# Turning the state-space values without TensorE, a third of the weight remainders on GpSimd, and a later row product in a two-layer hybrid decoder trunk

## The chip, the cores and the metric

The kernel runs on one core of a Trainium2 chip. The metric is the device time of one execution in microseconds (us), the median of several runs. Five engines work side by side, each with a queue of its own that it runs in order: TensorE (PE; its weight loads are listed as PEld), VectorE (DVE), ScalarE (ACT), GpSimd (POOL) and SyncE (SP), which here only issues DMAs. They wait for one another through semaphores. A name with a q behind it (SPq, ACTq) is the sequencer of that engine, which issues a DMA or waits.

## What is computed

Two layers run on a sequence of 512 rows of width 1024, in float32. Each layer norms its input, multiplies it by one large matrix, feeds four groups of heads, gates and joins them, multiplies by an output matrix, norms and adds.

```python
hn = rmsnorm(x, pre_g)
proj = hn @ w_in                                  # 1024 -> 6664
y_ret = retention(...) * silu(ret_g)
y_ssd = ssd_mixer(xbc, z, dt_raw, ...)            # state-space heads
y_sb  = stick_breaking(...) * silu(sb_g)
y_mem = memory_read(...) * silu(mem_g)
y = concatenate([y_ret, y_ssd, y_sb, y_mem]) @ w_out
return x + rmsnorm(y, post_g)

# in ssd_mixer, after the convolution and silu:
xs, bm, cm = split(xbc)
xdt = x_heads * delta                              # the values, by position
y_diag = einsum('bclsgj,bcsgjp->bclgjp', cb * decay_in, xdt)
states = einsum('bclgn,bclgjp->bcgjpn', bc, xdt * decay_states)
y = (y_diag + y_off) + x_heads * d_skip
y = rmsnorm((y * silu(z)) per group of 256, norm_g)
```

## The kernel before

Every float32 product of the large matrices is made of three matmuls. A tensor is held as a high part, rounded to the form that TensorE reads in one pass (fp32r), and a low part, the remainder (`x - high`); the product is high·high + high·low + low·high (`mm3`). ScalarE makes the high part by a copy (line 293), VectorE the low part by a subtraction (line 294), both in `split`.

**Weights.** They come from DRAM in 39 blocks a layer, each of two halves of 128 x 1024 (a few of 128 x 528); `w_load` loads a block of two into one of two `raw` buffers, `w_prefetch` splits a half into `wh` and `wl`. Halves are numbered k = 0 to 155 over both layers, 78 a layer. There are five buffers of `wh` and of `wl`, so half k can be split when half k-5 has been used, and in `proj_b` one half feeds 24 matmuls of 128 x 512. After an odd half has been split, its `raw` buffer is loaded anew from ScalarE's queue (line 353).

**Units.** `tick` counts one unit for each projection; `defer(n, f)` puts a step off until n units later. `ssd_group` (line 958) runs twice in each layer: two projections with a convolution make the values `X["x"]` (features by positions), further ones make B, C and the gates z. `ssd_values` (line 994) turns the values to positions by features: for each of two halves, four transposes of 128 x 128 on TensorE into a PSUM bank (line 1003), then VectorE multiplies by the step sizes into `xdt` (line 1007) and by the decay into `xds` (line 1009). `ssd_states` uses `xds` on TensorE one unit after the group's last projection, `ssd_out` uses `xdt` three units after it. `ssd_var` sums the squares over rows by a matmul and turns the row into reciprocal roots in `row_rstd` (ScalarE copy, DMA to 32 partitions, GpSimd add and power, DMA to DRAM, DMA back to all partitions); `ssd_norm` (line 1072) multiplies by them.

`columns_turned` (line 652) is the other way to turn a tile, used for B and for retention's keys: VectorE transposes blocks of 32 x 32 into a buffer (line 660), four DMAs put the 32-row strips into DRAM so that the blocks stand where they belong (line 663), and one DMA for each output reads it back (line 668), all on SP's queue.

`out_proj` multiplies the joined 16 tiles of 128 rows by the output matrix, column half by column half. In its first half tile kc is used by 12 matmuls; tiles 12 to 15 are the state-space outputs. At the end of layer 0 each quarter of the rows is normed (GpSimd adds and takes the power, lines 444, 449, 450), scaled (VectorE, line 470) and turned on TensorE (line 479) for the next layer.

Outside `start`, the order in each engine's queue is laid when the program is built, by a planner that takes whatever its own clock holds ready, in the order in which the steps are written (`schedule_with_timeline_sim=True`). Buffers come in tags with a fixed number of slots: "s" 33, "y" 16, "r" 9.

Of the kernel before, what the change touches and what calls it, by code (L numbers as in the profile page):

```python
# [8 lines left out]
F32 = mybir.dt.float32  # L9
# [7 lines left out]
P = 128  # L17
# [52 lines left out]
NBLK = len(BLOCKS)  # L70
# [4 lines left out]
def block_width(b):  # L75
    return 2 * (SUBD if BLOCKS[b % NBLK][0] == "d" else SUBW)
# [77 lines left out]

BLK = 32
TT = "y"
ST, SL, SB1, SB2 = "s", "y", 2, 4
ROW = 128  # L160

# [9 lines left out]
def v3(ap, a):  # L171
    return ap.rearrange("p (a b) -> p a b", a=a)


class Builder:
# [136 lines left out]
    def w_prefetch(self, upto=None, between=()):  # L312
        if self.starting and upto is None:
            return
        while self.w_split < (upto or min(self.nsubs, self.w_cur + self.NSUB)):
            k = self.w_split
            self.w_load(k // 2)
            n = block_width(k // 2) // 2
            h, l = (self.wp.tile([P, SUBW], F32R, tag=t, name=self.name(t), bufs=self.NSUB)[:, :n] for t in ("wh", "wl"))
            r = self.raw[k // 2]  # L320
            if isinstance(r, list):
                pieces = [(r[2 * (k % 2) + i][:], slice(512 * i, 512 * i + 512)) for i in range(2)]
            else:
                cs = [slice(0, n)] if k > 1 else [slice(0, n // 2), slice(n // 2, n)]
                pieces = [(r[:, (k % 2) * n + c.start:(k % 2) * n + c.stop], c) for c in cs]
            for i, (x, c) in enumerate(pieces):
                self.split(x, h[:, c], l[:, c], h[:, c].bitcast(F32))
                if i < len(between):
                    between[i]()
            self.sub[k] = (h, l)  # L330
            self.w_split += 1
            if k % 2:
                del self.raw[k // 2]
                if not self.starting:
                    self.w_load(k // 2 + self.NRAW)

    def w_load(self, b):
        while self.w_dma <= min(b, DEPTH * NBLK - 1):
            n = block_width(self.w_dma)
            src = self.a["wts"][self.w_off:self.w_off + P * n].rearrange("(p n) -> p n", p=P)  # L340
            if self.starting and self.w_dma == 2:
                r = [self.new(512, F32, "y") for _ in range(4)]
                for i in range(4):
                    self.nc.sync.dma_start(r[i][:], src[:, 512 * i:512 * i + 512])
            else:
                r = self.wp.tile([P, 2 * SUBW], F32, tag="raw", name=self.name("raw"), bufs=self.NRAW)
                if self.starting:
                    for c in ((slice(0, n),) if self.w_dma > 1 else (slice(0, n // 2), slice(n // 2, n))):
                        self.nc.sync.dma_start(r[:, c], src[:, c])  # L349
                        if not self.w_dma and not c.start:  # L350
                            self.mem_start()
                else:
                    self.nc.scalar.dma_start(r[:, :n], src)
            self.raw[self.w_dma] = r
            self.w_dma += 1
            self.w_off += P * n
# [273 lines left out]
    def mem_turn(self, h, w, y):  # L630
        nc = self.nc
        pT = []
        for m in range(2):
            T = self.buf(tag="y")
            for i in range(2):
                x = w[i].rearrange("p (t m j b) -> p m t j b", t=2, m=2, b=BLK)[:, m]
                nc.vector.transpose(T.rearrange("p (j t b) -> p t j b", t=NT, b=BLK)[:, 2 * i:2 * i + 2], x)
            d = self.turned_rows(P, SEQ)
            dd = d.rearrange("(j m) (a t) -> a m j t", m=BLK, a=P // BLK)
            pT.append(self.through_dram(T, dd, d, self.buf(tag="y")))  # L640
# [5 lines left out]
    def through_dram(self, T, dst, src, out):  # L646

        n = dst.shape[2]
        for a in range(P // BLK):
            self.nc.sync.dma_start(dst[a], v3(T[BLK * a:BLK * a + BLK], n))  # L650
        self.nc.sync.dma_start(out, src)
        return out

    def columns_turned(self, tiles, out):
# [3 lines left out]
        for k, x in enumerate(tiles):  # L658
            T = self.buf(n, TT)
            self.nc.vector.transpose(T, x)  # L660
            dd = d[:, P * k:P * k + P].rearrange("(b t) (a f) -> a t b f", t=BLK, a=P // BLK)
            for a in range(P // BLK):
# [296 lines left out]
    def ssd_group(self, l, g, ysb):  # L959

        X = {"l": l, "g": g}
        self.ssd_decay(X)
        X["x"] = [self.conv(self.proj_b(), 2 * g + i) for i in range(2)]
        self.defer(2, self.ssd_values, X)
        self.gated(("sb", 2 * g), ysb[2 * g])
        X["b"] = self.conv(self.proj_b(), 4 + g)
        X["bt"] = self.buf()[:, :3 * P]
        self.columns_turned([X["b"][:, :3 * P]], [X["bt"]])
        X["c"] = self.conv(self.proj_b(), 6 + g)
        self.defer(3, self.ssd_mix, X)  # L970
        self.gated(("sb", 2 * g + 1), ysb[2 * g + 1])
        X["y"] = [self.buf(tag="y"), self.buf(tag="y")]
        X["z"] = [self.gate(self.proj_b()) for _ in range(2)]
        self.defer(1, self.ssd_states, X)
        self.defer(3, self.ssd_out, X, 0)
        self.defer(3, self.ssd_out, X, 1)
        self.defer(5, self.ssd_var, X)
        self.defer(9, self.ssd_norm, X)

    def ssd_decay(self, X):  # L980
        nc, S = self.nc, self.ssd
# [12 lines left out]
    def ssd_values(self, X):  # L994

        nc, g = self.nc, X["g"]
        X["xdt"], X["xds"] = [], []
        for i in range(2):
            b = self.mx()
            for c in (2 * i, 2 * i + 1):  # L1000
                for j in range(2):
                    o = 256 * (c % 2) + P * j
                    nc.tensor.transpose(b[:, o:o + P], X["x"][j][:, P * c:P * c + P], self.con("ident", P))  # L1003
            xdt, xds = self.buf(), self.buf()
            for c in (2 * i, 2 * i + 1):
                s = slice(256 * (c % 2), 256 * (c % 2) + 256)
                nc.vector.tensor_tensor(out=v3(xdt[:, s], 4), in0=v3(b[:, s], 4), in1=self.per_head("delta", g, c), op=ALU.mult)
                if c < NT - 1:
                    nc.vector.tensor_tensor(out=v3(xds[:, s], 4), in0=v3(xdt[:, s], 4), in1=self.per_head("dst", g, c), op=ALU.mult)
            X["xdt"].append(xdt)  # L1010
            X["xds"].append(xds)
# [323 lines left out]
```

## Time and profile before

| | before |
|---|---|
| median of 3 runs | 924.06 us (923.71 to 925.14) |
| the profiled execution | 923.25 us |
| its span | 921.5 us |
| TensorE busy | 913.2 us, 99% |
| VectorE busy | 673.3 us, 73% |
| ScalarE busy | 443.5 us, 48% |
| GpSimd busy | 146.3 us, 16% |
| TensorE's granted clock | 0.998 of full speed |

The profile is of one execution. Its span is the time from the first instruction to the last; the execution's own time is 1.75 us longer. An engine is busy while it has an instruction in hand; matmuls overlap, each listed 0.39 us long for 512 columns but started 0.227 us apart, so what one costs is read from the start of the next.

### The profile page before, as it was taken

To read this page: it belongs to the slowest core of one execution; us is meant where nothing else is said; L and a number is where in the kernel's file an instruction comes from. 1 tells how busy PE (TensorE), PEld (TensorE's weight loads), DVE (VectorE), ACT (ScalarE), POOL (GpSimd) and SP (SyncE) were. 2 spreads that over 40 slices of the span, in tenths; PEclk is the share of its full clock that TensorE was granted. 3 is DMA by queue.
4 is the path that set the end of the run, shared out by engine and by line. 5 is a ranking of instruction groups with operands and counts; after the bars stand their busy time and mean duration, and the time that the engine had idled before them with its cause. 6 is when DMAs were issued, how large, how long until landed. Compare 5 with 4: busy or idle time off the path is not lost.

```text
span 921.5 us, 12952 instructions
## 1 busy us (share of the span) xinstructions
PE 913.2 (99%) x4667; PEld 773.6 (84%) x4667; DVE 673.3 (73%) x1081; ACT 443.5 (48%) x841; POOL 146.3 (16%) x208
## 2 busy tenths in 40 slices
PE   9999999999999999999999999999999999999997
PEld 7998888888888888888899888888888888888885
DVE  6855689888787887844587476898778869687343
ACT  6643485744453342733465336675445434335341
POOL 1200152320131110100040002423112120102001
PEclk9999999999999999999999999999999999999999
DMA  8544664642444333444345256556333362422502
GB/s 316 213 141 144 169 167 104 199 146 61 120 134 148 116 109 126 137 149 158 116 173 196 93 172 183 124 122 183 103 109 116 110 194 92 139 95 88 210 12 91
DMA packets 105408, 128.53 MB, mean 139 GB/s; under 512 B 64640, under 2 KB 79744, under 8 KB 96256
## 3 DMA queue, kind: packets, MB, share of 16 engines
q10 hardware_dynamic: 10224, 73.44, 23.4%
q1 hardware_dynamic: 95120, 54.28, 20.7%
q8 instruction: 36, 0.59, 0.3%
q14 instruction: 28, 0.23, 0.1%
HBM read 112.10 MB, written 15.56 MB: 139 GB/s over the span
## 4 chain that ended last, share of the span: by engine, by line
PE 98%; DMA 1%; ACT 0%; DVEq 0%; SPq 0%; POOLq 0%; issue 0%; POOL 0%; ACTq 0%; DVE 0%
PE pj L285 74%; PE mx L285 23%; PE mx L479 1%; DMA mem<-memT 1%; PE mx L1003 0%; ACT s L523 0%; DVEq L1331 0%; ACT s L1168 0%; POOLq L1331 0%; ACT wh L293 0%; SPq L506 0%; SPq L349 0%; SPq L1206 0%; POOL t L449 0%; ACTq L1331 0%
## 5 line engine op out<-in xcount | busy, mean ns | idle before, releaser
L285 PE MATMUL pj<-hTh,wh 128*128 128x512 f32 x704 | 276.4, 393 | 0.0
L285 PE MATMUL pj<-hTh,wl 128*128 128x512 f32 x704 | 275.8, 392 | 0.0
L285 PE MATMUL pj<-hTl,wh 128*128 128x512 f32 x704 | 274.6, 390 | 0.0
L294 DVE TENSOR_TENSOR wl<-raw,wh 128x1024 fp32r<-128x1024 f32 (+2 forms) x156 | 188.6, 1214 | 116.9 <-ACT wh L293 115.7
L293 ACT CAST wh<-raw 128x1024 fp32r<-128x1024 f32 (+2 forms) x156 | 158.7, 1020 | 205.0 <-PE pj L285 177.5
L285 PEld LDWEIGHTS pj<-hTh,wl 128*128 128x128 f32 x704 | 132.2, 188 | 27.3
L285 PEld LDWEIGHTS pj<-hTh,wh 128*128 128x128 f32 x704 | 132.3, 188 | 27.1 <-DVE s L593 0.8
L285 PEld LDWEIGHTS pj<-hTl,wh 128*128 128x128 f32 x704 | 132.3, 188 | 26.6
L285 PE MATMUL pj<-wh,s 128*128 128x512 f32 x320 | 97.6, 391 | 0.0
L285 PE MATMUL mx<-s,s 128*128 128x256 f32 (+4 forms) x528 | 79.7, 307 | 0.0
L285 PE MATMUL mx<-wh,s 128*128 128x512 f32 x256 | 79.2, 389 | 0.0
L285 PEld LDWEIGHTS mx<-s,s 128*128 128x128 f32 (+1 forms) x528 | 65.8, 177 | 8.2 <-PE pj L285 1.4
L285 PEld LDWEIGHTS pj<-wh,s 128*128 128x128 f32 x320 | 59.7, 188 | 12.4
L285 PE MATMUL pj<-wl,s 128*128 128x512 f32 x160 | 60.2, 389 | 0.0
L285 PEld LDWEIGHTS mx<-wh,s 128*128 128x128 f32 x256 | 48.1, 188 | 10.0
L294 DVE TENSOR_TENSOR s<-y,s 128x512 fp32r<-128x512 f32 x64 | 41.2, 687 | 19.7 <-ACT s L293 14.0
L262 ACT ACTIVATE s<-s 128x128 f32<-128x128 f32 (+3 forms) x96 | 41.8, 478 | 22.3 <-DVE s L733 20.6
L675 POOL TENSOR_TENSOR s<-y,s 128x512 fp32r<-128x512 f32 x16 | 23.7, 1494 | 179.9 <-ACT s L674 179.4
L293 ACT CAST s<-y 128x512 fp32r<-128x512 f32 x64 | 36.6, 617 | 30.8 <-PE mx L285 22.0
L285 PE MATMUL mx<-wl,s 128*128 128x512 f32 x128 | 49.6, 389 | 0.0
L285 PE MATMUL pj<-wl,hTh 128*128 128x256 f32 (+2 forms) x144 | 47.6, 331 | 0.0
L285 PE MATMUL pj<-wh,hTl 128*128 128x256 f32 (+2 forms) x144 | 47.5, 330 | 0.0
(185 smaller groups left out, 1298.5 us busy)
## 6 DMA issues: line engine op xcount, KB each, us to landing
raw<-wts ACTq DMA_DIRECT2D x69, 1024.0 KB, 4.8
s<-x SPq DMA_DIRECT2D x24, 256.0 KB, 4.1
y<-turned SPq DMA_DIRECT2D x24, 256.0 KB, 2.8
turned<-y SPq DMA_DIRECT2D x64, 64.0 KB, 2.2
s<-acs SPq DMA_DIRECT2D x16, 256.0 KB, 6.3
r<-row SPq DMA_DIRECT2D x12, 256.0 KB, 5.0
raw<-wts SPq DMA_DIRECT2D x4, 512.0 KB, 7.5
raw<-wts SPq DMA_DIRECT2D x2, 1024.0 KB, 6.3
```

What stands on the lines that cost most here:

```text
L262: i = self.nc.scalar.activation(out, in_, func, **k)
L285: return self.nc.tensor.matmul(out, lhsT, rhs, start=start, stop=stop)
L293: self.nc.scalar.copy(h, src)
L294: self.nc.vector.tensor_sub(l, src, hf)
L479: x = self.nc.tensor.transpose(b[:, P * j:P * j + P], hn[i][:, P * j:P * j + P], self.con("ident", P))
L675: nc.gpsimd.tensor_sub(p.l, x, p.hf)
```

## The change

The values are turned by `columns_turned` right after their convolutions, into two buffers of tag "r"; `ssd_values` loses its eight transposes and its PSUM banks, multiplies in place, and is put off by three units instead of two. The low part of every third weight half (k = 2, 5, 8, ... from 14 on, but not where k within its layer is 16 to 33) is formed by GpSimd instead of VectorE: 36 of 156 halves, 34 of them 1024 wide and two 528. `ssd_var` and `ssd_norm` are put off by two more units each.

```diff
+VD = 3
-TT = "y"
+TT, TX = "y", "r"
@@ w_prefetch
-                self.split(x, h[:, c], l[:, c], h[:, c].bitcast(F32))
+                nc = self.nc
+                nc.scalar.copy(h[:, c], x)
+                (nc.gpsimd if self.low_by_pool(k) else nc.vector).tensor_sub(l[:, c], x, h[:, c].bitcast(F32))
+    def low_by_pool(self, k):
+        return k > 12 and k % 3 == 2 and not 16 <= k % (2 * NBLK) < 34
@@ ssd_group
         X["x"] = [self.conv(self.proj_b(), 2 * g + i) for i in range(2)]
-        self.defer(2, self.ssd_values, X)
+        X["xt"] = [self.buf(tag=TX), self.buf(tag=TX)]
+        self.columns_turned(X["x"], X["xt"])
+        self.defer(VD, self.ssd_values, X)
-        self.defer(5, self.ssd_var, X)
-        self.defer(9, self.ssd_norm, X)
+        self.defer(7, self.ssd_var, X)
+        self.defer(11, self.ssd_norm, X)
@@ ssd_values
-            b = self.mx()
-            for c in (2 * i, 2 * i + 1):
-                for j in range(2):
-                    o = 256 * (c % 2) + P * j
-                    nc.tensor.transpose(b[:, o:o + P], X["x"][j][:, P * c:P * c + P], self.con("ident", P))
-            xdt, xds = self.buf(), self.buf()
+            b = xdt = X["xt"][i]
+            xds = self.buf()
```

## Rows read from the trace of the kernel before

**Rows 1.** The page, part 1: busy time, share of the span, instructions.
```profile
span 921.5 us, 12952 instructions
PE 913.2 (99%) x4667; PEld 773.6 (84%) x4667; DVE 673.3 (73%) x1081; ACT 443.5 (48%) x841; POOL 146.3 (16%) x208
```

**Rows 2.** The page, part 4: the chain that ended last, by engine.
```profile
PE 98%; DMA 1%; ACT 0%; DVEq 0%; SPq 0%; POOLq 0%; issue 0%; POOL 0%; ACTq 0%; DVE 0%
```

**Rows 3.** Waits of PEld: who waited for whom, us, times, longest.
```profile
PEld pj L285 <- DVE s L593: 0.8, 2, 0.4
...
PEld mx L285 <- DVE y L1082: 0.2, 1, 0.2
```

**Rows 4.** Line 1003: duration in ns (least/median/most), first and last start.
```profile
L1003 PE MATMUL mx<-consts,s x32: 270/272/273, 268.5 to 775.4; 128*128 128x128 f32 x32
```

**Rows 5.** Timeline of PE at 273 us: start, length, what.
```profile
273.04 0.71 PE L1003 MATMUL mx<-consts,s 128*128 128x128 f32 x5
...
273.82 0.39 PE L285 MATMUL pj<-hTl,wh 128*128 128x512 f32 x1
```

**Rows 6.** Groups of DVE by line and shape: busy us, mean ns | idle before.
```profile
L294 DVE TENSOR_TENSOR wl<-raw,wh 128x1024 fp32r<-128x1024 f32 x144 | 180.5, 1257 | 111.5 <-ACT wh L293 110.4
...
L1007 DVE TENSOR_TENSOR s<-mx,t 128x256 f32<-128x256 f32 x16 | 6.0, 417 | 1.2 <-PE mx L1003 1.2
...
L745 DVE STREAM_TRANSPOSE s<-s 128x512 f32<-128x512 f32 x8 | 5.5, 689 | 3.3 <-POOL s L736 3.3
```

**Rows 7.** Timeline of POOL in the stick-breaking stretch: its subtractions.
```profile
124.30 4.13 POOL L675 TENSOR_TENSOR s<-y,s 128x512 fp32r<-128x512 f32 x2 [0.82 <-ACT s L674]
...
150.62 1.30 POOL L759 TENSOR_TENSOR s<-y,s 128x512 fp32r<-128x512 f32 x1 [7.17 <-ACT s L758]
...
154.10 0.74 POOL L759 TENSOR_TENSOR s<-y,s 128x256 fp32r<-128x256 f32 x1
```

**Rows 8.** Timeline of DVE at 257 us, while POOL works beside it.
```profile
257.56 1.65 DVE L294 TENSOR_TENSOR wl<-raw,wh 128x1024 fp32r<-128x1024 f32 x1
```

**Rows 9.** Timeline of DVE and PE: one weight half of the middle, split and first used.
```profile
298.04 1.23 DVE L294 TENSOR_TENSOR wl<-raw,wh 128x1024 fp32r<-128x1024 f32 x1 [0.61 <-ACT wh L293]
...
326.19 0.39 PE L285 MATMUL pj<-hTh,wl 128*128 128x512 f32 x1
```

**Rows 10.** Timeline of ACT and PE: the last weight half (k = 155), high part, first use.
```profile
896.78 1.04 ACT L293 CAST wh<-raw 128x1024 fp32r<-128x1024 f32 x1
...
901.95 0.39 PE L285 MATMUL mx<-wl,s 128*128 128x512 f32 x1
```

**Rows 11.** Timelines of POOL, DVE, PE at the layers' border.
```profile
476.62 2.06 POOL L444 TENSOR_SCALAR t<-t 128x1 f32<-128x1 f32 x1 [2.55 <-ACT s L462]
...
479.64 1.41 DVE L470 SCALAR_TENSOR_TENSOR s<-s,t,s 128x512 f32<-128x512 f32 x2 [0.44 <-POOL t L450]
...
484.80 1.03 PE L479 MATMUL mx<-consts,s 128*128 128x128 f32 x8
```

**Rows 12.** Line 663's DMAs (issue ns; landing us); issues by kind; timelines at 269 to 299.
```profile
L663 SPq DMA_DIRECT2D turned<-y x48: 303/451/1466, 195.5 to 789.5; - x48
...
DMA to landing us min/median/max: 1.5/2.9/5.7
...
y<-turned SPq DMA_DIRECT2D x24, 256.0 KB, 2.8
...
269.43 0.69 DVE L943 SCALAR_TENSOR_TENSOR s<-s,s 128x512 f32<-128x512 f32 x1 [0.76 <-ACT s L267]
...
294.32 0.83 SPq L818 DMA_DIRECT2D r<-row  x2
...
298.80 2.35 PE L285 MATMUL mx<-s,s 128*128 128x128 f32 x14
```

**Rows 13.** Timelines of DVE and PE in the first half of layer 0's output product.
```profile
394.66 1.41 DVE L1075 SCALAR_TENSOR_TENSOR y<-y,consts,r 128x512 f32<-128x512 f32 x2 [3.69 <-DMA r<-row]
...
413.61 0.61 PE L285 MATMUL pj<-wh,s 128*128 128x512 f32 x2
```

## The prediction

> **What bounds the kernel now.** I read the busy times first: TensorE is busy for 913.2 of 921.5 us, VectorE for 673.3, GpSimd for 146.3 [rows 1]. Busy is not yet bound, since matmuls overlap in the list, so the chain comes next: 98% of it is TensorE behind itself [rows 2]. Then the waits: of all that TensorE waited for VectorE, weight loads included, there are five lines, from 0.8 us down to 0.2 [rows 3], 2.2 us together. The few other waits lie in the start. So between about 9 us and the last matmul TensorE runs without a hole, and each instruction taken from it should be worth the interval from its start to the next start. What is off TensorE counts only if it makes TensorE wait; for that I read, for each edit, how long before its use a result is ready.
>
> **The transposes.** There are 32 on line 1003 [rows 4]. Listed as 0.27 us each they would be 8.7 us, but they overlap. Five start at 273.04, and after them, past one 512-column matmul, the next starts at 273.82 [rows 5]: 0.78 us, less 0.235 for the matmul (the usual 0.227 and a few ns), gives 0.109 for one. At the other places where they stand the starts give 0.109 as well, also where only two stand between projections, so there is no further cost of changing over. Gain: 32 x 0.109 = **3.49 us**, all on the path.
>
> On VectorE a 32 x 32-block transpose of 512 columns costs 0.689 [rows 6]; two for each of four groups are 5.5 us. The multiplications stay seven for each group; reading SBUF instead of PSUM, I take them at the same 0.417 [rows 6] (line 1009 reads SBUF at this length already). All this lies on VectorE, at 73%, so it costs nothing as long as the states are in time. The new wait is theirs: VectorE's multiplication waits for the read back from DRAM, and behind it in VectorE's queue stand convolutions and weight remainders, which TensorE wants 10 to 28 us later. The wait for `r<-row` at line 1075 was 3.69 us at 394.66 [rows 13], and TensorE did not notice.
>
> How late is the read? The second values tile is ready at 269.43 + 0.69 = 270.1 in group 0 [rows 12]. Two transposes bring it to 271.5. Eight strip writes are issued by SP at 0.45 each (3.6 us), land 2.9 later, two reads are issued at 0.4 each and land after 2.8 [rows 12]: 281.6. Seven multiplications (2.9) make 284.5. Upper bound: writes and reads both take 5.7, the longest landing of line 663 [rows 12]: 271.5 + 3.6 + 5.7 + 0.8 + 5.7 + 2.9 = 290.2; what SP may add by being held is the third rival below. TensorE starts the group's states after eight small matmuls from 298.80 on [rows 12], 298.80 + 8 x 0.109 = 299.7. Spare: 9.5 to 15 us. I take 0 for the wait. The other SP work moved behind these ten DMAs (B's turning, the decay rows) is used at 299.7 or later too, and ten issues are 4.4 us of SP.
>
> The Trainium skill speaks against this edit: "VectorE: DVE Perf Modes", Rules for kernel authors, gives a transpose of 128 x 128 to TensorE where PSUM will do. By that rule the time would stay at the median of before; the rows speak for the edit, since here TensorE is the only full engine.
>
> **The low parts.** 36 halves go from VectorE to GpSimd: 34 at 1.257 us [rows 6] and two at half width, 44 us off VectorE. On GpSimd no subtraction of 1024 columns is shown. Undisturbed, 512 take 1.30 and 256 take 0.74 [rows 7]: 2.2 ns a column, so 1024 make 1.30 + 512 x 0.0022 = 2.4 us (estimate). Disturbed by VectorE, two of 512 took 4.13 [rows 7], 1.6 times as long, and the worse of them 1.76 times: 4.3 us for 1024. GpSimd gains 85 to 150 us and stays under a third. A low part thus comes 1.2 to 3.1 us later. The middle of the kernel has room: one split at 298.04 is done at 299.3 and first used at 326.19 [rows 9], 27 us ahead, and from k = 35 to 71 I find 15 us or more. The tightest moved half is the last, 155: its high part ends at 897.8, its low part is wanted at 901.95 [rows 10], 4.1 us for a work of 2.4, with VectorE idle and nothing in GpSimd's queue until 906. Cost 0; at 4.3 us it would be 0.2.
>
> Loading a `raw` buffer also waits for an odd half's low part, on ScalarE's queue: 1.2 us later where GpSimd makes it, against some 10 us of lead. Cost 0.
>
> VectorE and GpSimd do hinder each other: a subtraction of VectorE that takes 1.22 alone took 1.65 at 257.56 [rows 8], and a GpSimd add of a single column took 2.06 at 476.62 [rows 11], against 0.2 beside an idle VectorE. So I give the second rival below more than half of what remains beside the forecast in the faster cases. The Trainium skill, "SBUF — State Buffer", SBUF: two separate sides, says more: a VectorE operation with two SBUF inputs and a GpSimd operation that reads SBUF lock each other out for a whole instruction. The two rows agree in kind; the first shows 0.43 lost, not a whole instruction. By that rule VectorE could lose up to 34 x 2.4 = 82 us instead of winning 44 and would still be under 80% busy, so only the second rival would gain by it.
>
> **The row product later.** In the last group two units are 4 tiles of the output product, 48 matmuls of 0.227: 10.9 us. The normed tiles are there at 394.66 + 1.41 = 396.1, and with some 1.4 us for ScalarE's and VectorE's split of the first one of them at 397.5; tile 14 is wanted at 413.61 [rows 13]. Spare 16.1, after the change 5.2. GpSimd's power may stand behind one low part (2.4 to 4.3), which leaves 0.9 at worst. Cost 0, without much room.
>
> **Sum.** 921.5 - 3.5 = 918.0 of span, 919.8 for the profiled execution. That one lies 0.8 below the median of the runs (923.25 against 924.06), so the median should be 924.06 - 3.49 = **920.6**.
>
> **Rivals.** *The queues are laid differently.* The planner lays every queue anew, and a matmul that stood safe may stand ahead of its data. No row shows the price; what TensorE waited for VectorE before, 2.2 us [rows 3], bounds it both ways: all of it gone 918.4, as much again 922.8. For it: every edit moves VectorE's and SP's work. Against: nearly all waits of the old order are under 0.4.
>
> *The border of the layers gives back part.* There GpSimd's adds and powers make the chain to the transposes of line 479, and low parts of k = 83 and 86 (ready at 467 and 476) now stand among them. In the third quarter line 470 ends at 481.05 and the transposes start at 484.80 [rows 11]: 3.7 us of room, in the second quarter 2.7. One low part at its worst, 4.3 us, is over by 0.6 to 1.6: 921.2 to 922.2; two in a row double it, up to 923.8. Against: VectorE is relieved of just these halves.
>
> *SP holds the values back, and the kernel is slower.* If SP's reads of the turned values stand behind the second reciprocal row (SP issues its last DMA at 294.32 to 295.2 [rows 12]), they are issued at 295.2, land 2.8 to 5.7 later, and the multiplications end at 301.7 to 304.6 with the issues: TensorE waits 2.0 to 4.9 us in group 0 of each layer, 4 to 10 in all: 924.6 to 930.4, 929 in the likelier case of crowded DMA. It decides from a read issued later than 293.4 (then twice 2.7 us exceed the 3.5 gained by over 0.2%). For it: SP runs strictly in order and already waits for this row. Against: the read is due 10 us earlier.
>
> **How the numbers follow.** Forecast, 919.8 to 921.6: 0.55. Laid better, 918.4 to 919.8: 0.07. Border or new order give back up to half, 921.6 to 922.2: 0.16 (its faster part with that of the first rival). They give back about all, 922.2 to 925.9: 0.12. SP or a like wait, above: 0.10. About 0.2%, 1.9 us, is what a measurement can tell from no change; so faster 0.78, same 0.12, slower 0.10. The range 919.2 to 923.2 leaves out the slowest cases, half of those within 0.2% and half of the better order: some 0.19.
>
> **What would show it.** Right: no line 1003 on TensorE; busy near 909.7; waits for VectorE still near 2 us; low parts on GpSimd near 2.4 us; VectorE near 635 us. Wrong: TensorE waiting ahead of line 1031 (states) or for `xt`, an SP queue that issues the reads after 293, waits ahead of line 479 between 465 and 490, or a hole at tile 14 of either output product.

## The result and the profile after

| | before | after |
|---|---|---|
| median, beside one another (19 runs each) | 922.88 us (922.16 to 925.14) | 925.56 us (922.91 to 928.17) |
| ratio, with its 95% interval | | 1.0030 (1.0022 to 1.0039) |
| the profiled execution, its span | 923.25, 921.5 us | 925.56, 923.8 us |

The changed kernel is 0.3% slower, where 0.4% faster was forecast: 2.7 us lost in place of 3.5 gained. Line numbers of after are about seven above those of before (the row's steps of `row_rstd` are 815 to 825, the values' multiplications 1012 and 1014, the retention row's sum and remainder 873 and 879).

The page of after, to be read against [rows 1, 2]: the busy line, and the chain that ended last.

```profile
PE 910.6 (99%) x4635; PEld 771.0 (83%) x4635; DVE 662.4 (72%) x1053; ACT 440.9 (48%) x841; POOL 238.3 (26%) x244
PE 95%; DMA 3%; DVE 1%; SPq 0%; ACT 0%; POOL 0%; issue 0%; DVEq 0%; POOLq 0%; ACTq 0%
```

TensorE has its 32 instructions less and is busy for 2.6 us less; 3.5 less was forecast, and a slower clock, below, makes up most of the difference. DMA now has 3% of the chain, where it had 1%. The waits of TensorE (engine and line that waited, what for, us in total, times, longest) show where, beside [rows 3]:

```profile
PE mx L286 <- DVE r L879: 4.5, 2, 2.3
PEld mx L286 <- issue: 6.7, 10, 2.7
```

The second line is in the main the weight loads of the same two products (2.65 and 2.67 us). Line 879 was in no list before. It is the remainder of retention's second row of squares; its product is one matmul of `onesr`. TensorE's start-to-start intervals put the two holes at 288.90 and 743.31, 2.42 and 2.43 us over the usual interval, one in each layer.

**What VectorE did ahead of the first hole** (start, duration, line, operation; in brackets the idle time before it and what ended it):

```profile
281.30 0.57 DVE L667 STREAM_TRANSPOSE y<-s 128x384 f32<-128x384 f32 x1
287.14 0.76 DVE L1012 TENSOR_TENSOR r<-r,t 128x256 f32<-128x256 f32 x2 [5.27 <-DMA r<-turned]
287.91 0.68 DVE L873 TENSOR_TENSOR r<-r 32x512 f32<-32x512 f32 x1
288.79 1.22 DVE L330 TENSOR_TENSOR wl<-raw,wh 128x1024 fp32r<-128x1024 f32 x1 [0.20 <-DVE r L873]
289.94 0.75 DVE L1012 TENSOR_TENSOR r<-r,t 128x256 f32<-128x256 f32 x2
290.72 0.68 DVE L879 TENSOR_TENSOR r<-r,r 32x512 fp32r<-32x512 f32 x1
```

VectorE stands idle for 5.27 us at the first multiplication of the values, which waits for their read from DRAM. The row's last sum (873) and its remainder (879) stand behind it and have nothing to do with the values. From the landing (287.04) to the end of line 879 it takes 4.4 us; the product was due at 288.90 + 0.23 = 289.13, so TensorE waits 287.04 + 4.4 - 289.13 = 2.3 us.

**What SP did ahead of that** (the DMAs as they are issued), first in after:

```profile
266.76 1.96 SPq L670 DMA_DIRECT2D turned<-y  x4
268.82 1.24 SPq L818 DMA_DIRECT2D t<-r  x2
273.07 0.85 SPq L670 DMA_DIRECT2D turned<-y  x2
275.03 0.50 SPq L822 DMA_DIRECT2D row<-t  x1
275.58 0.58 SPq L670 DMA_DIRECT2D turned<-y  x1
279.71 1.23 SPq L825 DMA_DIRECT2D r<-row  x2
280.99 0.43 SPq L670 DMA_DIRECT2D turned<-y  x1
284.35 0.88 SPq L675 DMA_DIRECT2D r<-turned  x2
```

and in a kernel with the values turned and the row product put off, but no low part on GpSimd (e5 below, 919.52 us):

```profile
264.95 1.24 SPq L818 DMA_DIRECT2D t<-r  x2
267.37 1.98 SPq L670 DMA_DIRECT2D turned<-y  x4
270.70 0.50 SPq L822 DMA_DIRECT2D row<-t  x1
271.30 1.06 SPq L670 DMA_DIRECT2D turned<-y  x2
272.46 0.93 SPq L825 DMA_DIRECT2D r<-row  x2
273.43 1.38 SPq L670 DMA_DIRECT2D turned<-y  x2
279.67 1.28 SPq L675 DMA_DIRECT2D r<-turned  x2
```

The rows `t<-r`, `row<-t`, `r<-row` belong to retention's first row of reciprocal roots. In e5 they go ahead of the values' strips; in after four strips go first, GpSimd's power starts 4 us later (271.63 against 267.76), and `row<-t` is issued at 275.03. (Why the planner puts them first is not shown: a relieved VectorE may have the first transpose ready earlier by the planner's clock, which no trace holds.) At 274.19 ScalarE has issued a weight load of 1 MB. The DMAs issued around these times (KB each, median us from issue to landing), after and then e5:

```profile
raw<-wts ACTq DMA_DIRECT2D x1, 1024.0 KB, 5.3
...
row<-t SPq DMA_DIRECT2D x1, 4.0 KB, 4.7
```

```profile
raw<-wts ACTq DMA_DIRECT2D x1, 1024.0 KB, 5.4
...
row<-t SPq DMA_DIRECT2D x1, 4.0 KB, 1.7
```

The 4 KB of `row<-t` land after 1.7 us where they are issued ahead of the weight load, and after 4.7 where they are issued behind it. SP may not read the row before it has landed, and it runs in order: from 276.16 to 279.71 it stands, with the last strip behind it. So the values are read at 284.35 and not at 279.67, 4.7 us later; in e5 line 879 ended 2.4 us before its product was due, and 4.7 - 2.4 is the hole.

**The rest of the difference** is TensorE's clock behind the first hole. TensorE in after, then windows of it (length, busy us of PE, PEld, DVE, ACT and POOL with their instructions, the granted clock as a share of full speed, DMA share, GB/s):

```profile
288.68 0.39 PE L286 MATMUL pj<-hTh,wl 128*128 128x512 f32 x1
288.90 0.39 PE L286 MATMUL pj<-hTh,wh 128*128 128x512 f32 x1
291.55 0.59 PE L286 MATMUL mx<-r,onesr 128*2 128x512 f32 x1 [2.26 <-DVE r L879]
291.93 0.63 PE L286 MATMUL pj<-hTl,wh 128*128 128x512 f32 x1
292.36 0.63 PE L286 MATMUL pj<-hTh,wl 128*128 128x512 f32 x1
```

```profile
284.00:288.00 4.00, 4.00 (x20) 3.30 (x18) 0.85 (x3) 0.00 (x0) 0.00 (x0) 1.00 0.67 169
292.00:295.00 3.00, 3.00 (x9) 2.39 (x8) 2.98 (x5) 0.19 (x1) 0.00 (x0) 0.54 0.74 300
746.00:749.00 3.00, 3.00 (x14) 2.50 (x15) 3.00 (x6) 0.61 (x1) 0.00 (x0) 1.00 0.75 306
```

Behind the hole the matmuls start 0.43 apart and not 0.227: the clock granted from 292 to 295 is 0.54, about the lower of its two levels (1.2 and 2.4 GHz). Seven matmuls of 512 columns ran so, from 291.55 on, and lost 1.3 us together. Behind the hole of layer 1 the clock stayed at 1.00. The sum for the profiled executions: -3.5 for the transposes, +4.85 for the holes, +1.3 for the clock, +2.65; the spans differ by 2.3, the medians by 2.7. How much the clock takes differs from one execution of after to the next: the two with a mean granted clock of 0.999 and 1.000 took 922.91 and 923.31 us, the seven with 0.995 took 926.75 to 928.17; the profiled one has 0.998.

### The profile page after: what moved, and what is told of

It is laid out like the page before. It is cut to its first block, busy times and chain, and to the rows that moved or that the text cites. A ratio compares the mean times of both kernels' runs of the same rounds, so it can differ in the third digit from the quotient of the medians.

```text
span 923.8 us, 12978 instructions
## 1 busy us (share of the span) xinstructions
PE 910.6 (99%) x4635; PEld 771.0 (83%) x4635; DVE 662.4 (72%) x1053; ACT 440.9 (48%) x841; POOL 238.3 (26%) x244
## 4 chain that ended last, share of the span: by engine, by line
PE 95%; DMA 3%; DVE 1%; SPq 0%; ACT 0%; POOL 0%; issue 0%; DVEq 0%; POOLq 0%; ACTq 0%
PE pj L286 71%; PE mx L286 23%; DMA row<-t 1%; PE mx L486 1%; DMA turned<-y 1%; DMA mem<-memT 1%; DMA r<-turned 1%; DVE r L1012 0%; DVE wl L330 0%; SPq L825 0%; POOL t L820 0%; DVE r L879 0%; DVE r L873 0%; ACT s L530 0%; DVEq L1336 0%
## 5 line engine op out<-in xcount | busy, mean ns | idle before, releaser
L330 DVE TENSOR_TENSOR wl<-raw,wh 128x1024 fp32r<-128x1024 f32 (+2 forms) x120 | 147.2, 1230 | 81.4 <-ACT wh L329 70.0
L330 POOL TENSOR_TENSOR wl<-raw,wh 128x1024 fp32r<-128x1024 f32 (+1 forms) x36 | 89.4, 2484 | 266.8 <-ACT wh L329 266.8
L286 PE MATMUL mx<-s,s 128*128 128x256 f32 (+3 forms) x400 | 71.9, 316 | 0.0
L286 PEld LDWEIGHTS mx<-s,s 128*128 128x128 f32 x400 | 59.2, 190 | 6.4 <-issue 1.4
L295 DVE TENSOR_TENSOR s<-y,s 128x512 fp32r<-128x512 f32 x64 | 49.3, 815 | 19.9 <-ACT s L294 14.1
```

The lines of the kernel that those rows point to most:

```text
L286: return self.nc.tensor.matmul(out, lhsT, rhs, start=start, stop=stop)
L295: self.nc.vector.tensor_sub(l, src, hf)
L330: (nc.gpsimd if self.low_by_pool(k) else nc.vector).tensor_sub(l[:, c], x, h[:, c].bitcast(F32))
```

## The experiments

Ratios are against the kernel before, run beside each; its median was 922.5 to 922.9 us in all of them.

### e1 and e2: each half of the change alone

e1 is the kernel before with the low parts on GpSimd:

```diff
-                self.split(x, h[:, c], l[:, c], h[:, c].bitcast(F32))
+                nc.scalar.copy(h[:, c], x)
+                (nc.gpsimd if self.low_by_pool(k) else nc.vector).tensor_sub(l[:, c], x, h[:, c].bitcast(F32))
...
+    def low_by_pool(self, k):
+        return k > 12 and k % 3 == 2 and not 16 <= k % (2 * NBLK) < 34
```

> The kernel before with the one edit that every third weight half's low part is formed by GpSimd; the values are turned on TensorE as before, the row product stands where it stood. Theory A (what TensorE lost lies in the turning: VectorE waits at the multiplication for a read that SP issues late, and the retention row product stands behind it): within 0.1% of the kernel before, 922 to 924 us, no hole on TensorE near 289 or 743 us. Rival B (the low parts on GpSimd do it, by the shared port or by delaying GpSimd's power): 2 to 4 us slower than before, with holes.

924.58 us, ratio 1.0024 (1.0014 to 1.0033): slower, by a little less than Rival B had it.

e2 is the kernel after with all low parts on VectorE and the row product at its old place:

```diff
-        return k > 12 and k % 3 == 2 and not 16 <= k % (2 * NBLK) < 34
+        return False
...
-        self.defer(7, self.ssd_var, X)
-        self.defer(11, self.ssd_norm, X)
+        self.defer(5, self.ssd_var, X)
+        self.defer(9, self.ssd_norm, X)
```

> The change without the low parts on GpSimd and with the row product where it stood before: only the values turned by VectorE and DRAM. Theory A: VectorE waits 4 to 6 us for the turned values in the first group of each layer, TensorE has a hole of 1 to 3 us there in each layer, and the time is 923 to 926 us against 922.9 of the kernel before. Rival B (GpSimd's low parts delay the power and so SP): no hole, 3.5 us faster than before, 919.4.

920.06 us, ratio 0.9973 (0.9963 to 0.9983): the turned values gain 2.7 us by themselves, and Theory A, that the turning itself loses the time, falls. The two halves add to -0.9; together they make +2.7. So neither price is the sum's; something of 3.6 us arises between them. e1's waits are at another place than after's, VectorE's last additions for the states of group 0 (line 1040 there). This profile is of the slowest of its ten executions, 928.77 us:

```profile
PE mx L286 <- DVE s L1040: 2.0, 2, 1.4
```

There the rows of the decay, 256 KB each, come to VectorE late (those of group 1 landed 306.5 to 309.0, before 302.15 to 304.5), and VectorE stands at their subtraction with the states' additions behind it.

### e3 and e4: what stands behind the wait, and SP relieved of the row

e3, on the kernel after, puts the multiplications of line 1012 behind the remainder of line 879:

```diff
+        self.zsub = nc.vector.tensor_sub(z[r + 32:r + 64], sq[0:32], z[r:r + 32].bitcast(F32))
...
+                m = nc.vector.tensor_tensor(out=v3(xdt[:, s], 4), in0=v3(b[:, s], 4), in1=self.per_head("delta", g, c), op=ALU.mult)
+                self.behind(m, self.zsub)
```

> The changed kernel with one edit: VectorE's four multiplications of the turned values are ordered behind the last VectorE step of the retention row product. SP's queue keeps the order up to the reads, so the values still land near 287 us. Theory A: TensorE's holes at 289 and 743 us are gone, also the half clock behind the first; 3.5 us faster than the kernel before, 919 to 920. Rival C (the late read reaches TensorE in another way, by the states or by the convolutions behind the multiplication): a hole of 1 to 3 us moves elsewhere, 922 to 925.

925.69 us, ratio 1.0034 (1.0021 to 1.0047). The holes went on by one step, to 294.4 and 747.7 us, where the convolution of C (line 950) stands behind the same wait:

```profile
PE mx L286 <- DVE s L950: 4.3, 2, 2.4
```

But the values did not come back as in after. VectorE's weight remainder no longer stands behind the wait, so the next 1 MB of weights is issued at 283.43 and not at 290.09, 0.2 us ahead of the values' read (283.66), and that read lands after 5.8 us, at 289.43:

```profile
283.43 0.33 ACTq L360 DMA_DIRECT2D raw<-wts  x1
289.52 1.43 DVE L1012 TENSOR_TENSOR r<-r,t 128x256 f32<-128x256 f32 x4 [5.45 <-DMA r<-turned]
```

In layer 1 it takes 6.0. In e6, with no load beside it, it takes 2.6. By these times the values would have come 3.1 and 3.4 us earlier without the load, more than the holes of 2.1 and 2.6 (estimate). So e3 does not show that a new order of VectorE alone moves the hole; its second load beside the read is enough for it.

e4 issues the row's write and reads from ScalarE:

```diff
-        nc.sync.dma_start(d.rearrange("o (p j) -> (o p) j", j=RJ), c)
+        nc.scalar.dma_start(d.rearrange("o (p j) -> (o p) j", j=RJ), c)
...
-            nc.sync.dma_start(out[i], d[i:i + 1].to_broadcast([P, SEQ]))
+            nc.scalar.dma_start(out[i], d[i:i + 1].to_broadcast([P, SEQ]))
```

> The changed kernel with the reciprocal rows' write to DRAM and their reads back issued on ScalarE's queue instead of SP's, VectorE's order left to the planner. Theory A with SP as the cause of the late read: the strips are issued without a break and the values land near 281 to 284 instead of 287; the hole shrinks by 3 us or more to nothing; 919 to 921 us. Rival D (the DMA itself is slow, SP's order matters little): the values land near 287, hole of 2 us as in the changed kernel, 924 to 926. ScalarE now waits for these rows; if that stalls the high parts, a new hole shows.

928.46 us, ratio 1.0066 (1.0045 to 1.0088). The hole at 289 is gone and that at 743 is down to 0.68, but there are others at 310.0 and 765.0 (2.10 each, the additions for the states) and at 337.2 (1.46). It moved every other queue as well, and a weight load issued at 274.76 stood just ahead of the values' read (275.60, landed after 5.8), so it told where the waits could go rather than what caused them.

### e5 and e6: is it the later row product?

e5 is e2 with `ssd_var` and `ssd_norm` at 7 and 11; e6 is the kernel after with them at 5 and 9.

> The kernel after with all low parts on VectorE again: the values are turned by VectorE and DRAM, and the row product stands two units later. Base for comparison is the kernel with the values alone (920.06 us, row product at its old place). Theory L (the low parts on GpSimd are what costs, the later row product costs nothing): 919 to 921, one hole of about 2 us at the normalisation's row product (336 us) gone or smaller, none at 289 and 743. Theory V (the later row product turns the gain of the values into a loss): 923 to 926, with the holes at 289 and 743 us of the kernel after.

919.52 us, ratio 0.9970 (0.9958 to 0.9981); holes 0.77 us in all. (In e2's profile, 921.57 us, there is one of 2.0 at 335.9, before the row product at its old place.)

> The kernel after with the row product at its old place: values turned and low parts on GpSimd. Theory L: 923.5 to 927, that is holes of about 2 us in the state-space stretch of both layers as in the low parts alone. Theory V: 919 to 921. If the two edits simply added, it would be 920.06 + 1.8 = 921.9.

925.40 us, ratio 1.0033 (1.0022 to 1.0045), holes of 2.25 and 2.29 at 288.3 and 741.7. So the later row product costs nothing (919.52 beside 920.06), and it is the low parts that turn the gain of the values round.

### e7 and e8: GpSimd's work, or VectorE's relief?

Both have the values turned and the row product at 5 and 9. In e7 VectorE makes all low parts, and GpSimd makes copies of the 36 that nobody reads; in e8 the 36 low parts are left out:

```diff
+        self.scr = self.fixed(480, BF16, "scr")
...
+                nc.vector.tensor_sub(l[:, c], x, h[:, c].bitcast(F32))
+                if self.low_by_pool(k):
+                    w = min(480, (c.stop - c.start) // 2)
+                    for o in (0, w):
+                        nc.gpsimd.tensor_sub(self.scr[:, :w], x[:, o:o + w], h[:, c][:, o:o + w].bitcast(F32))
```

```diff
+                if self.low_by_pool(k):
+                    l = h
+                else:
+                    nc.vector.tensor_sub(l[:, c], x, h[:, c].bitcast(F32))
```

> The values turned, row product at its old place, VectorE makes all low parts as before, and GpSimd makes a second copy of the 36 low parts into a scratch tile that nobody reads (two subtractions of 480 columns in bfloat16 for each). So GpSimd has the work and VectorE is not relieved. Theory P (what costs is GpSimd's work itself: it holds up VectorE's instructions, and GpSimd's other steps stand behind it): 922 to 926, VectorE's subtractions longer than in the kernel with the values alone, holes of TensorE in the state-space stretch. Theory R (what costs is that a relieved VectorE gives another laid order, in which TensorE's small products stand ahead of their data): 919 to 921.5.

939.39 us, ratio 1.0181 (1.0166 to 1.0196).

> The values turned, row product at its old place, and the 36 low parts are left out: their products take the high part a second time, so the output is not the reference's. VectorE is relieved of 44 us and GpSimd has nothing more to do. Theory P: 918.5 to 920.5, no more holes than the kernel with the values alone. Theory R: 922 to 926, with holes of about 2 us in the state-space stretch.

926.77 us, ratio 1.0053 (1.0031 to 1.0076). Its profile, of the slowest of five executions (930.60 us), has a hole of 2.26 at 288.7 like after's; its counterpart in layer 1 is only 0.39, and more is lost before the last additions for the states (line 1041 there), 1.9 at 313.1 and 0.8 and 1.9 at 767.5 and 768.8:

```profile
PE mx L286 <- DVE s L1041: 4.5, 3, 1.9
PE mx L286 <- DVE r L882: 2.3, 2, 2.1
```

So a VectorE that is only relieved, with nothing given to GpSimd, is enough for slower queues and for the hole of layer 0. But e7 shows that GpSimd's work without relief does harm too, and more (holes of 4.7 us at 338.9 and 799.7 and of 1.4 at 287.8 and 748.6, not traced further); neither theory had foreseen 939. What e7 and e8 have in common is that the planner laid the queues anew: against e2, the order differs on every engine's queue, in e8 on all but GpSimd's. e8's SP order has three strips ahead of `t<-r`, and its `row<-t`, issued at 271.87 with the weight load at 271.98, landed 5.7 us later.

### e9 and e10: SP's order alone

e9 is the kernel after with the row's DMAs ahead of the strips on SP, much as in e5. All other queues are, instruction by instruction, those of after:

```diff
-                self.nc.sync.dma_start(dd[a], v3(T[BLK * a:BLK * a + BLK], n // BLK))
+                w = self.nc.sync.dma_start(dd[a], v3(T[BLK * a:BLK * a + BLK], n // BLK))
+                if len(tiles) == 2:
+                    self.behind(w, self.row if k else self.tr)
...
+            self.tr = nc.sync.dma_start(c[RP * i:RP * i + RP], e[i:i + 1].rearrange("o (p j) -> o p j", j=RJ))
...
+        self.row = nc.sync.dma_start(d.rearrange("o (p j) -> (o p) j", j=RJ), c)
```

> The kernel after with one thing changed: on SP the retention row's two writes t<-r stand ahead of the first values tile's four strips, and its row<-t ahead of the second tile's strips. Every other engine's queue is, instruction by instruction, that of the kernel after, with all low parts on GpSimd. Theory S (SP's order is the cause: the row's write comes behind the weight load of 274 us and holds SP for 4.7 us, so the values come back 4 us late): row<-t lands about 2 us after its issue, the values are read at about 280, the holes at 289 and 743 us (4.85 us together) and the half-clock matmuls behind the first (1.4) go: 919 to 921. Theory R (TensorE's small products stand ahead of their data in the new order of TensorE and VectorE): that order is unchanged, so 923 or more, with the holes at the same or the next product. Theory P (GpSimd's low parts hold up VectorE): 923 or more as well.

923.40 us, ratio 1.0005 (0.9993 to 1.0018): 2.2 us better than after by that alone, though not all of it; Theory S had 919 to 921, and the time by itself fits R and P as well (923 or more). The rows decide for layer 0: `row<-t` now lands 1.7 us after its issue in both layers, and the hole of layer 0 is 0.76, the order of all other queues unchanged. That of layer 1 is still 2.60:

```profile
724.52 0.49 SPq L824 DMA_DIRECT2D row<-t  x1
725.06 0.59 SPq L670 DMA_DIRECT2D turned<-y  x1
726.21 0.81 SPq L827 DMA_DIRECT2D r<-row  x2
727.07 1.91 SPq L670 DMA_DIRECT2D turned<-y  x3
735.02 0.90 SPq L677 DMA_DIRECT2D r<-turned  x2
```

The weight load went out at 724.93, so now the strips themselves land late, behind it and behind the row's two reads (731.73 and 734.10): the last at 734.89. The sum worked out above holds for both: landing of the values plus 4.4, less the time at which the product is due, is 284.63 + 4.4 - 288.37 = 0.7 and 737.71 + 4.4 - 739.61 = 2.5.

e10 is the reverse: e5, that is no low part on GpSimd, with SP's order of after forced on it (`t<-r` behind the first tile's strips, `row<-t` between the second tile's). The other queues are nearly those of e5:

```diff
...
+                if self.rows and k and a > 1:
+                    self.behind(w, self.rows[a - 2])
+            if self.pending and len(tiles) == 2:
+                f, a = self.pending
+                self.rows, self.pending = f(*a, w), None
...
+            if w:
+                self.behind(t, w)
...
```

> The reverse: the kernel with the values turned and the later row product but no low part on GpSimd (919.5 us), with SP's order of the kernel after forced on it: t<-r behind the first tile's strips, row<-t behind two strips of the second, one strip, the two r<-row, the last strip, then the reads. The other engines' queues are the same but for one matmul in each layer, which changes places with its neighbour. Theory S: holes of about 2 us at 287 and 740 us, 922.5 to 925. Theories R and P: 919 to 920.5, no hole there, since neither VectorE nor GpSimd has other work.

929.48 us, ratio 1.0072 (1.0055 to 1.0089): 10 us slower than e5, by the order of thirteen DMAs in each layer and what the planner made of it. (More than one matmul moved: three instructions of VectorE and two of ScalarE in each layer changed places with neighbours as well, one weight remainder to ahead of the states' last addition. e9 is the cleaner of the two.) There are holes of 0.97 and 1.03 at the product of after's line 879 (289.4 and 744.9; line 897 there), about half of what Theory S had, and, what had not been expected, of 1.9 at 312.0 and 767.6 and of 1.55 at 795.6 (the row product of the state-space group):

```profile
PE mx L287 <- DVE s L1056: 3.7, 2, 1.9
PE mx L287 <- DVE r L897: 1.7, 2, 0.9
```

Line 1056 there is line 1040 of e1, the additions for the states, and the reason is that of e1: the rows of the decay land later (307.4 to 310.2, in e5 303.6 to 306.0), and VectorE stands before them.

### e11 and e14: low parts outside the state-space stretch

Ten of the 36 low parts fall into the state-space stretch of the layers. They go back to VectorE, in the kernel after (e11) and in e1 (e14):

```diff
-        return k > 12 and k % 3 == 2 and not 16 <= k % (2 * NBLK) < 34
+        return k > 12 and k % 3 == 2 and not 16 <= k % (2 * NBLK) < 34 and not 45 <= k % (2 * NBLK) < 62
```

> The kernel after without the low parts on GpSimd that fall into the state-space stretch of each layer (ten halves go back to VectorE; 26 stay on GpSimd). SP's queue is then that of the kernel without any low part on GpSimd. Theory S, and R as well: 918.5 to 920.5, no hole at 289 and 743. If the other 26 low parts cost something by themselves (hindering of VectorE, the border of the layers, the last half): 921 to 924, with waits outside the state-space stretch.

920.37 us, ratio 0.9982 (0.9969 to 0.9995), no hole at 289 and 743, 0.77 us of holes in all. SP's order is e5's.

> The kernel before (values turned by TensorE), with only the 26 low parts outside the state-space stretch on GpSimd. If the cost of the low parts alone (1.8 us) comes from the ten inside the stretch: 922 to 923.3, the time of before within 0.05%. If low parts cost wherever they stand: 923.5 to 924.6.

922.96 us, ratio 1.0003 (0.9993 to 1.0012), no hole: the time of before. The 26 low parts outside the stretch neither cost nor gain anything that these runs can tell; the ten inside cost 1.6 us alone and 5.2 with the turned values (925.56 against 920.37).

### e12 and e13: nothing behind the wait

e12, on the kernel after, puts all multiplications of line 1012 behind line 879 and behind the convolution of C, one unit later; e13 does so for group 0 alone (its edit; e12's has no `if`):

```diff
-VD = 3
+VD = 4, 3
...
+                if not g:
+                    self.behind(m, self.zsub)
+                    self.behind(m, self.convd)
```

> The kernel after with VectorE's seven multiplications of each group put behind the retention row's remainder and behind the convolution of C (and written one unit later). SP still has the order of the kernel after, so the values still come back at about 287, but VectorE has nothing for TensorE behind that wait any more. The planner then places the row product six matmuls earlier, so its data have to be there 1.4 us sooner. Theory S with the last link at the head of VectorE's queue: no hole at 289 and 743, nor at 294 and 748; the multiplications end at about 295, ahead of the states at 300: 919 to 921. If a late value read costs TensorE in any order, the hole moves to the states at 296 to 300 us or stays: 923.5 to 927.

930.57 us, ratio 1.0083 (1.0066 to 1.0099). Neither theory had this. The longest holes are of 1.9 at 346.1 and 801.9 and of 1.5 at 790.5.

> As the run before, but for group 0 alone: its multiplications stand behind the retention row's remainder and the convolution of C, those of group 1 stay as in the kernel after. All low parts on GpSimd as in the kernel after, and SP's order up to the read of group 0's values as well, so these values still come late (at 286 to 291). Theory S, with the wait at the head of VectorE's queue as its last link: no hole at 289, 294, 743 or 748, and none in group 1 beyond those of the kernel after (none): 919 to 921.5. If a late read costs TensorE in any order: 924 or more, holes at the states of group 0 (297 to 303).

928.66 us, ratio 1.0058 (1.0042 to 1.0075). In both the holes at 289, 294, 743 and 748 are gone, though the values came back even later than in after, at 291.30 in e12 and 290.19 in e13, each read issued just behind a weight load as in e3. That settles the last link of after's holes: a late read costs TensorE there because VectorE waits for it with TensorE's own data behind. But the time is not won. In e13 TensorE waits 3.5 and 8.1 us at 334 and 791, for the row product of the state-space group itself (line 1075 there). VectorE ahead of the second (the profiled execution is the slowest of five, 935.27 us):

```profile
787.42 0.68 DVE L958 SCALAR_TENSOR_TENSOR s<-s,pj 128x512 f32<-128x512 f32 x1
789.27 0.76 DVE L1012 TENSOR_TENSOR r<-r,t 128x256 f32<-128x256 f32 x2 [1.16 <-DMA r<-turned]
792.91 0.76 DVE L1012 TENSOR_TENSOR r<-r,t 128x256 f32<-128x256 f32 x2 [2.88 <-DMA r<-turned]
...
798.21 0.69 DVE L1075 TENSOR_TENSOR r<-r,r 64x512 fp32r<-64x512 f32 x1
```

It is the same pattern once more, at group 1's values: their second read, issued at 787.10, 0.1 us behind a weight load, landed at 792.89. Earlier, at 764 and 768, VectorE stood for 1.5 and 3.6 us before the rows of the decay. The place of the wait can be moved; the number of DRAM reads for which VectorE waits with other work behind it stays.

## Why the prediction was wrong

**The transposes were right.** Their price of 3.49 us is about what e5 shows: its last matmul ends 2.90 us earlier than before's, and it has 0.77 us of holes that before does not have, 3.67 together.

**The step that failed is the wait put at 0.** It cost 4.85 us of holes and 1.3 of clock behind the first, which make up nearly all of the 6.2 us between forecast and result. The sum said of VectorE's new wait that behind it stand convolutions and weight remainders which TensorE wants 10 to 28 us later. Behind it stood also the remainder of retention's row, which TensorE wanted 2.4 us after its own end in e5. The spare of 9.5 to 15 us was worked out for the states, and there it held: no wait at the states in after. It was not worked out for what VectorE's queue holds behind the waiting instruction. The arrival of the values was forecast for 281.6; without low parts on GpSimd it was 282.24 and 283.87 (e5), with them 287.04 and 287.93. The upper bound of 290.2 was for the end of the multiplications, so 287.3 for the arrival, and neither held: in after the last multiplication ended at 292.5. The states, at 300.8, did not wait all the same. Two terms of that sum were too short: the second tile's transpose ended at 273.04 and not 271.5, and the last strip was issued 8 us behind that, since SP waited for the 4 KB of `row<-t` behind a load of 1 MB. No row of before shows that order of SP, but before's trace does show the price: its `row<-t` issued at 798.27, 1.1 us behind such a load, took 3.8 us.

**The third rival had the mechanism, with the wrong row and threshold.** It made SP's reads stand behind the second reciprocal row, gave 2.0 to 4.9 us a layer, and let it decide from a read issued later than 293.4. It was the first row, and a read issued at 284.35 was enough for 2.42 us (at 738.68 for 2.43), since line 879 and not the states was short of time behind it. With all like waits it had a chance of 0.10.

**The first rival had the cause, and its price was no bound.** "The planner lays every queue anew" is what e7 and e8 show, and e9 and e10 that an order alone costs time. It was bounded by the 2.2 us that TensorE waited for VectorE before [rows 3], as much again at most. But waits of an old order say nothing of a new one's: here 4.85 us of holes, in e10 7.4.

**The low parts.** 2.4 us was near, as the first of these groups of after shows, with 2.53 on the mean (operation, shape and count, busy us, mean ns, idle time before):

```profile
L330 POOL TENSOR_TENSOR wl<-raw,wh 128x1024 fp32r<-128x1024 f32 x34 | 86.0, 2528 | 263.7 <-ACT wh L329 263.7
L295 DVE TENSOR_TENSOR s<-y,s 128x512 fp32r<-128x512 f32 x64 | 49.3, 815 | 19.9 <-ACT s L294 14.1 <-PE mx L286 5.6
```

So was the cost 0 for their own lateness: no wait for a low part, at the last half or elsewhere, in after and e14. What was not seen is that to relieve VectorE, which was put at no cost, gives other queues and another order of SP (e8; with the ten low parts of the state-space stretch back on VectorE, e11, SP's order is that of e5 again). VectorE was forecast at some 635 us and has 662.4: it is relieved of 37.7 us where nobody makes the 36 low parts (e8 637.7, against 675.4 in e2), and gets 24.7 of them back as longer instructions once GpSimd does (e6, 662.4). The second group is one place of it: 815 ns on the mean, against 687 in before and 688 in e8.

**The border of the layers** showed no wait of TensorE; the second rival did not come to pass. Nor did the later row product cost anything (e5).

**What stays open.** Why e9 keeps a hole of 2.60 in layer 1 is told by its rows; that another place of the weight load would take it away was not tried. In e4, e7 and e12 the further holes were read off, but not traced back one by one. By what rule the planner chose these orders no run shows.

The best of these kernels are e5, 919.52 us, e2, 920.06, and e11, 920.37, too near to one another to rank: the values turned, and either no low part on GpSimd or none within the state-space stretch.

## What to carry to other kernels

Where an engine gets a new wait for a DMA, list what stands behind it in that engine's queue and when each of these is wanted; the spare of the waiting instruction's own consumer is not the spare of the wait. Where a planner lays the order, work taken from an engine off the path need not be free: it can change which DMAs go first, and an edit that "costs nothing" should first be tried away from the stretch that is tight. Before a small DMA round trip (write, read back) is costed, look for the large load that is issued beside it, and remember that to free an engine can bring that load forward (e3).

## What the runs showed of the hardware

**A small write lands when the large load ahead of it does.** In the 16 traces 79 writes `row<-t` of 4 KB were issued while a load of 1 MB (5.3 us) that another engine had issued was on its way; 70 of them landed 0.14 to 0.27 us behind it, as in after 4.7 us after their issue. Of the 49 others 47 took 1.3 to 2.1 us; the two left, in e8, took 5.5 and 5.7, with a load issued 0.1 us behind them. A read of the values, 256 KB, took 2.6 us by itself (e6) and 5.5 to 6.6 beside such a load (e3, e12, e13). The Trainium skill, "DMA: Bandwidth & Descriptors", Issuing engines are not separate DMA queues, says that DMAs of all issuing engines run on the same 16 engines and interleave. These rows agree: a load from ScalarE's queue holds back a write from SP's by up to 4 us.

**One GpSimd instruction can stop VectorE for most of its length.** In after, two multiplications of VectorE, then the GpSimd subtraction beside them:

```profile
298.46 3.46 DVE L893 TENSOR_TENSOR y<-y,r 128x512 f32<-128x512 f32 x2
```

```profile
298.47 2.91 POOL L330 TENSOR_TENSOR wl<-raw,wh 128x1024 fp32r<-128x1024 f32 x1 [19.82 <-ACT wh L329]
```

Two such multiplications take 1.28 us in before, so 2.2 us are lost to one subtraction of 2.9; the second multiplication alone takes 2.86. On the average of the 36 it is 24.7 / 36 = 0.7 us, and beside 17 of them VectorE's instructions last no longer than their medians. The Trainium skill, "SBUF — State Buffer", SBUF: two separate sides, speaks of a lock for the whole instruction; this place agrees with it better than the row that the prediction leant on (0.43 us, [rows 8]).

**A hole of 2.4 us can halve the clock behind it, and need not.** Behind the hole at 288.9 the granted clock was 0.54 for some 3 us, about 1.3 us lost; behind one of the same length at 743.3 it stayed at 1.00. In e1 a hole of 1.5 us at 766.3 had 0.50 behind it, from 768.2 to 771.4.
